# Linear attention's decays computed in pieces between the gates, sigmoids applied later, projections in another order

## The chip, the cores and the metric

The kernel runs on one core of a Trainium2 chip. The metric is the device time of one launch in microseconds (us). The engines are TensorE (PE in the profile; its weight loads are PEld), VectorE (DVE), ScalarE (ACT), GpSimd (POOL) and SyncE (SP), which issues most of the DMAs here.

## The reference

One layer of a streaming encoder on 16 meta tokens and 1024 frames, model width 1024, all in float32. The part around the change is the middle of it:

```
h += 0.5 * swiglu(rmsnorm(h))                       # first feed-forward block
u  = rmsnorm(h) * mix_norm
aq, ak, av, gq, gk, gv, gr, g_low, gate_a, gate_b = split(u @ w_in)
A  = window attention(aq, ak, av)                   # 8 heads, 2 kv heads, chunks of 64
log_a = log_sigmoid(g_low @ gla_gate_w + gla_gate_b) / 16
b  = cumsum(log_a) within a chunk                   # decays of linear attention
qe = gq/8 * exp(b);  ke = gk * exp(-b)
o  = causal(qe ke^T) v + qe S;   S' = exp(b_last) * S + (gk * exp(b_last - b))^T v
B  = rmsnorm(o) * silu(gr)
h += (sigmoid(gate_a) * (A @ Wa) + sigmoid(gate_b) * (B @ Wb)) @ w_out
h += 0.5 * swiglu(rmsnorm(h))                       # second feed-forward block; then a last rmsnorm
```

Linear attention has 4 heads with keys of 64 and values of 128. q, k and the decays are two tiles of 128 rows (two heads each, p = 0 and 1), gv and gr four tiles each, the gates sixteen.

## The kernel before

Everything is kept transposed: 128 features on the partitions, tokens along the free dimension. A float32 product is made of three matmuls, high x high, high x low and low x high, where "high" is the operand cast on ScalarE and "low" the rest, subtracted on VectorE (`split`, `Weights.cut`, `Seven.halves`).

The kernel is one program with unrolled loops. The tile framework orders it: it puts each engine's instructions into that engine's queue in an order of its own, by the program's order where operands are there, and derives the semaphores from the buffers. Each queue is worked off in order. A pool of tiles has a fixed count of buffers for a tag; a new tile waits until an old one's last reader is done.

The stages in order, by their lines:

1. The first feed-forward block, up to 704.7 us, in products of Strassen's kind with seven in place of eight (`Seven`, L453). Its last part is the loop at L819 to L848: for each half c of the tokens (520 each) and each of the eight tiles m, matmuls of the last hidden rows (L827) into a double PSUM bank, the residual sum `add_half` (L340, VectorE), a store, the square (L834, ScalarE) and the sum of squares (L836, VectorE or GpSimd). The norm's scale of the first half (`scales_of_half`, `scales_to_rows`) and the first scaled inputs (`scaled`, L807 to L811) lie within the second half's turns.
2. Plain projections. The PSUM pool of four double banks is closed and a pool of eight banks opened. `together` (L901) runs projections of several tiles and chunks of tokens side by side over the eight k tiles, with hooks between: K0, K1 and V0 of linear attention, and later V1. `ev_keep` copies a tile to DRAM, `ev_tok` copies a tile of V and later transposes it by tokens (L888, L892, on TensorE) and stores that. Between them VectorE makes the differences of tokens (L935 to L938) and their halves (L229) for the next stage.
3. Gates: `gate_pair` (L958) for m = 0, 2 to 14, again seven products of 12 matmuls of 512 columns each, into three accumulators (pb, pa, pd). Between the products, copies and sums take the accumulators out; a sigmoid on ScalarE (L973) follows and a store to `gates`.
4. Attention: its own projections first, then a loop over 16 chunks of 64 frames. Each turn has transposes of the probabilities, the scores of the next chunk with its softmax (VectorE, ScalarE, VectorE), a slot of filling work for TensorE, and the product with V. The slots hold V2 and V3, the two Q tiles and the four R tiles of linear attention, and the low-rank projection (`low_rank`) in slot 9.
5. Linear attention (`Gla`). `decays` (L1360 to L1391) for a whole head pair: z = gate matmul, Abs, Exp, Ln, the running sum (scan, L1373) and four more Exp, with products on VectorE and GpSimd. `begin` transposes the scaled keys (L1398, L1404), `products` (L1422), `step` (L1429 to L1443), `end`. Units of the attention branch (`branch_units`, 12 matmuls each, L96 to L98) fill the turns: five before the first head, then one in each turn of the first and in the even turns of the second as long as more than two are left. `out_gate` multiplies with Silu of gr.
6. The branch of linear attention (`ev_b`), the output projection, and the second feed-forward block.

Of the kernel before, what the change touches and what calls it, by code (L numbers as in the profile page):

```python
# [17 lines left out]
P = 128  # L18
D = 1024
KT = D // P  # L20
# [15 lines left out]
def hybrid_kernel(  # L36
# [13 lines left out]

    def bank(name="ps"):
        return psp.tile([P, 512], F32, tag="ps", name=name)
# [415 lines left out]
    dbl = {}  # L468
# [345 lines left out]
    wt = Weights([w_more, w_main, w_main], [r_main])  # L814
    plain_views = [cols_view(w_in, c) for c in (C_GK, C_GK + P, C_GV, C_GV + P)]
    raws = [wt.raw(v) for v in plain_views[0:2]]
    hw = [None] * 4
    dgs = {}
    for c in range(2):  # L819
        for m in range(KT):  # L820
# [12 lines left out]
            sq = sqs[m % 3][:, c * N1:(c + 1) * N1] if m else accs[c]  # L833
            nc.scalar.activation(sq, hm, AF.Square)  # L834
            if m:
                (nc.vector if c == 0 or m >= KT - 2 else nc.gpsimd).tensor_add(accs[c], accs[c], sq)  # L836
            if c == 0 and m in (1, 3):
                hw[m // 2] = ktiles(wt.cut(raws[m // 2], eng=nc.gpsimd))
            if c == 1:
                if m == 1:  # L840
                    raws.append(wt.raw(plain_views[2]))
# [36 lines left out]
    def ev_tok(i):  # L878

        def evac(ps, c0, n):  # L880
# [4 lines left out]
            def turn():  # L885
# [3 lines left out]
                nc.vector.tensor_copy(g[:, 0:fr * P], pt[:, 0:fr * P])  # L889
                nc.sync.dma_start(out=gv_dram[i, :, c0:c0 + fr * P], in_=g[:, 0:fr * P])  # L890
                if c0 + n == T:
                    nc.tensor.transpose(pt[0:NM, fr * P:fr * P + P], v[:, n - NM:n], ident)  # L892
                    nc.vector.tensor_copy(g[0:NM, fr * P:fr * P + P], pt[0:NM, fr * P:fr * P + P])
                    nc.sync.dma_start(out=gvm_dram[i], in_=g[0:NM, fr * P:fr * P + P])

# [3 lines left out]
    plain_evac = [ev_keep(gk_dram[0]), ev_keep(gk_dram[1]), ev_tok(0), ev_tok(1)]  # L899

    def together(tiles, chunks, hooks=()):  # L901

        pss = [(i, c0, n, bank("pj")) for i in tiles for c0, n in chunks]
# [9 lines left out]
        run_late()  # L913
        for i, c0, n, ps in pss:
            plain_evac[i](ps, c0, n)

    def second_scales():
        dgs[1] = scales_of_half(1, bank("tot"))

    hooks = {k: (lambda k=k: scaled(k, 0)) for k in range(3, KT)}  # L920
    hooks[2] = second_scales
    together([0, 1], CH_T[0:1], hooks)
    scales_to_rows(1, (bank("rep"), bank("rep")), dgs[1])
    for m in range(KT):
        scaled(m, 1)
    together([2], CH_T[0:1])
    together([0, 1, 2], CH_T[1:])
    ra.close()
    t_r = g7.enter_context(tc.tile_pool(name="tr", bufs=8, side="right"))
    g8 = Seven("mx", 512, lambda kind, which, turn: bank(f"p{kind}"), (t_r, t_g, blk, None, w_more), None, None, None, N1)  # L930
# [11 lines left out]
    hw[3] = ktiles(wt.cut(wt.raw(plain_views[3])))  # L942
    for ch in CH_T:
        together([3], [ch])
    run_late()
# [12 lines left out]
    def gate_pair(m):  # L958
# [13 lines left out]
        def keep(i, c, to, src):  # L972
            nc.scalar.activation(to, src, AF.Sigmoid)  # L973
            nc.sync.dma_start(out=gates[m + i, :, c * 512:(c + 1) * 512], in_=to)
# [7 lines left out]
        keep(0, 0, x11, x11)  # L982
# [7 lines left out]
        keep(1, 1, x22, x22)  # L990
        product(5)
        nc.vector.tensor_add(x12, d, x12)
        keep(0, 1, x12, x12)
        product(6)
        keep(1, 0, g8.block("x21"), b)
# [10 lines left out]
    wt.ws = [w_main]  # L1006

# [66 lines left out]


    GR = 2 * NM
    gw, glow = qp.tile([3 * GR, 256], F32R, name="gw"), qp.tile([P, T], F32R, name="glow")
    gwf = ttile("gwf")[0:3 * GR, 0:256]
    for i in range(6):
        nc.gpsimd.dma_start(out=gwf[i * NM:(i + 1) * NM, :], in_=gla_gate_w)  # L1080
    nc.scalar.copy(gw, gwf)
    nc.vector.tensor_sub(gw[2 * GR:, :], gwf[2 * GR:, :], gw[2 * GR:, :].bitcast(F32))

# [152 lines left out]

    def low_rank():
        raw = wt.raw(cols_view(w_in, C_GL, NM))
        w2 = w_main.tile([P, 1024], F32R, tag="w", name="w2", align_bytes=128)[:, 0:KT * 2 * NM].rearrange("p (k m) -> p k m", k=KT)
        rv = raw[:, 0:KT * NM].rearrange("p (k m) -> p k m", k=KT)  # L1240
        nc.scalar.copy(w2[:, :, 0:NM], rv)
        nc.vector.tensor_sub(w2[:, :, NM:2 * NM], rv, w2[:, :, 0:NM].bitcast(F32))
        for c0, n in CH_ALL:
            ps = bank("pj")
            for k in range(KT):
                nc.tensor.matmul(ps[0:2 * NM, 0:n], w2[:, k, :], u_hi[k][:, c0:c0 + n], start=(k == 0), stop=False)
                nc.tensor.matmul(ps[0:2 * NM, 0:n], w2[:, k, :], u_lo[k][:, c0:c0 + n], start=False, stop=(k == KT - 1))
            a = ps[0:GR, 0:n]
            hi = glow[0:GR, c0:c0 + n]
            nc.scalar.copy(hi, a)  # L1250
            nc.scalar.copy(glow[2 * GR:3 * GR, c0:c0 + n], a)
            nc.vector.tensor_sub(glow[GR:2 * GR, c0:c0 + n], a, hi.bitcast(F32))
# [5 lines left out]
    for i in range(2):  # L1258
        slots += [[u] for u in project_units(cols_view(w_in, C_GQ + i * P), CH_FR, ev_keep(gq_dram[i], 0.125))]
    for i in range(4):  # L1260
        slots += [[u] for u in project_units(cols_view(w_in, C_GR + i * P), CH_FR, ev_keep(gr_dram[i]))]
    slots[9].append(low_rank)
    values(0)
    cur = scores(0)
    held[0]()
    held[1]()
    for c in range(16):
        nxt = None
        turn(cur)
        if c < 15:  # L1270
            nxt = scores(c + 1)
        if c % 2 == 0 and c < 14:
            values(c // 2 + 1)
        for u in slots[c]:
            u()
        attend(cur)
        cur = nxt
    run_late()
    att.close()

# [26 lines left out]
    def load_a(m, c0, n):  # L1307
        g = ttile("ga")
        nc.sync.dma_start(out=g[:, 0:n], in_=gates[m, :, c0:c0 + n])
        return g  # L1310

    def ev_a(ps, m, c0, n, g):
        nc.vector.tensor_mul(g[:, 0:n], ps[:, 0:n], g[:, 0:n])
        nc.sync.dma_start(out=gates[m, :, c0:c0 + n], in_=g[:, 0:n])
# [3 lines left out]
    for m0 in range(0, KT, 2):  # L1318
        views = [(slice(g * 64, g * 64 + 64), lambda r: r.rearrange("p (k m) -> p k m", k=4),
                  w_branch_att[g * 256:(g + 1) * 256, m0 * P:(m0 + 2) * P].rearrange("(i d) m -> d i m", d=64)) for g in range(2)]  # L1320
        fill += branch_units(views, ya, m0, load_a, ev_a)

# [7 lines left out]
    for p in range(2):  # L1330
        for x, src, n in (("k", gk_dram[p], T), ("q", gq_dram[p], S), ("v", gv_dram[2 * p], S), ("w", gv_dram[2 * p + 1], S)):
            ins[x, p] = atile(f"g{x}{p}")
            nc.sync.dma_start(out=ins[x, p][:, 0:n], in_=src)
# [9 lines left out]
    reset = gp.tile([P, T], F32, name="reset", bufs=1)  # L1343
    nc.gpsimd.memset(reset, 1.0)
    nc.gpsimd.memset(reset.rearrange("p (a b) -> p a b", b=16)[:, 0:65:8, 0:1], 0.0)
    ssq = gp.tile([P, 2, 8, 2], F32, name="ssq", bufs=1)
# [373 lines left out]
```

## Time and profile before

| | |
|---|---|
| median of 3 runs | 2061.68 us (2061.63 to 2062.08) |
| profiled execution | 2064.81 us |
| its span, first to last instruction | 2063.1 us |
| mean granted TensorE clock | 0.987 |
| DMA | 334.62 MB, mean 162 GB/s |

The stages' bounds in the span are about 729.5 (first projection), 794.5 (first gate), 946.9 (attention's projections), 1003 (chunks), 1166.6 (linear attention) and 1266.6 us (its branch). In a table of stretches each row has the stretch, its length, then the busy time and the count of instructions of PE, PEld, DVE, ACT and POOL, the granted clock, the DMA share and the rate. A row of the waits has who waited, for whom, the sum in us, how often, and the longest. A row of a group has its line, engine, operation, out<-in with shapes and count, then busy us and mean ns, then the idle time before it with its releasers. Matmuls overlap in their pipeline, so a matmul's own duration is longer than the distance to the next one.

### The profile page before, as it was taken

The page shows a single profiled execution, that of the slowest core. Times are in us where ns is not written, and L with a number is a line of the kernel's source. Part 1 is how long each engine was busy: PE and PEld are TensorE (multiplying, and loading weights), DVE is VectorE, ACT ScalarE, POOL GpSimd, SP SyncE. Part 2 cuts the span into 40 slices and gives each one's busy share as a digit, 9 for nine tenths or more (in the row PEclk, how much of TensorE's full clock was granted, in tenths as well). Part 3 has the DMA queues.
Part 4 walks back from the last instruction along what each step waited for, and adds up shares of the span by engine and source line. Part 5 has one row for each costly group of instructions (what it writes and reads, how often), then busy time and mean ns, then how long its engine had stood idle before and what let it go on. Part 6 is the DMA issues. An engine that isn't in the chain of part 4 may idle for free.

```text
span 2063.1 us, 31910 instructions
## 1 busy us (share of the span) xinstructions
PE 2011.8 (98%) x12084; PEld 1784.1 (86%) x12084; DVE 1397.7 (68%) x2393; ACT 873.6 (42%) x1692; POOL 197.8 (10%) x216
## 2 busy tenths in 40 slices
PE   8899999999999999999999989999999999999998
PEld 8899999999999987888888767888888888878888
DVE  5866677676678785443466668668876776757885
ACT  5534444444322353433466635344544544442222
POOL 1000000001222110005000100120000000022212
PEclk9999999999999999999999989999999999999999
DMA  6333344349975323335111454741544443599822
GB/s 204 107 108 131 125 162 159 124 153 344 349 289 202 99 92 109 108 107 136 44 58 57 154 168 147 260 140 51 170 167 132 168 157 126 199 372 345 287 92 82
DMA packets 280874, 334.62 MB, mean 162 GB/s; under 512 B 25094, under 2 KB 190720, under 8 KB 280720
## 3 DMA queue, kind: packets, MB, share of 16 engines
q1 hardware_dynamic: 263072, 271.18, 39.8%
q10 hardware_dynamic: 17296, 61.29, 8.0%
q8 instruction: 95, 1.56, 0.3%
q14 instruction: 59, 0.48, 0.1%
q0 software_dynamic: 352, 0.11, 0.1%
HBM read 216.45 MB, written 116.06 MB: 161 GB/s over the span
## 4 chain that ended last, share of the span: by engine, by line
PE 87%; DVE 5%; DMA 4%; ACT 2%; issue 1%; POOL 0%; SPq 0%; DVEq 0%; POOLq 0%; ACTq 0%
PE pb L453 34%; PE pd L453 17%; PE pa L453 8%; PE pj L96 2%; PE pj L97 2%; PE pj L98 2%; PE wo L96 1%; PE wo L98 1%; PE wo L97 1%; PE br L96 1%; PE br L98 1%; PE br L97 1%; PE pd L827 1%; PE pg L628 1%; PE pg L630 1%
## 5 line engine op out<-in xcount | busy, mean ns | idle before, releaser
L453 PE MATMUL pb<-tt,wop 128*128 128x260 f32 (+1 forms) x2208 | 385.2, 327 | 0.0
L453 PEld LDWEIGHTS pb<-tt,wop 128*128 128x128 f32 x2208 | 330.9, 188 | 35.5
L229 DVE TENSOR_TENSOR wop<-s,wop 128x512 fp32r<-128x512 f32 x264 | 186.5, 713 | 113.3 <-ACT wop L228 112.7
L228 ACT CAST wop<-s 128x512 fp32r<-128x512 f32 x264 | 161.4, 622 | 226.0 <-PE pb L453 90.2
L453 PE MATMUL pb<-tm,wop 128*128 128x260 f32 (+1 forms) x1440 | 237.3, 321 | 7.1 <-DVE h L340 4.5
L453 PEld LDWEIGHTS pb<-tm,wop 128*128 128x128 f32 x1440 | 209.5, 190 | 27.2 <-DVE h L340 5.0
L228 ACT CAST wop<-raw 128x512 fp32r<-128x512 f32 x198 | 122.5, 623 | 223.6 <-PE pb L453 105.4
L229 DVE TENSOR_TENSOR wop<-raw,wop 128x512 fp32r<-128x512 f32 x198 | 139.5, 709 | 20.2 <-ACT wop L228 19.9
L436 POOL TENSOR_TENSOR s<-raw 128x512 f32<-128x512 f32 x28 | 37.1, 1326 | 1060.5 <-DMA tm<-f1mid 454.9
L453 PE MATMUL pd<-tt,wop 128*128 128x260 f32 (+1 forms) x768 | 136.4, 329 | 0.0
L453 PEld LDWEIGHTS pd<-tt,wop 128*128 128x128 f32 x768 | 115.9, 188 | 13.1
L340 DVE SCALAR_TENSOR_TENSOR h<-pb,h 128x520 f32<-128x520 f32 (+1 forms) x136 | 94.0, 693 | 39.8 <-PE pb L453 37.7
L453 PE MATMUL pd<-tm,wop 128*128 128x260 f32 (+1 forms) x720 | 118.8, 319 | 0.0
L453 PE MATMUL pb<-tb,wop 128*128 128x260 f32 (+1 forms) x672 | 112.3, 320 | 0.5 <-ACT vec L87 0.5
L453 PEld LDWEIGHTS pd<-tm,wop 128*128 128x128 f32 x720 | 104.3, 188 | 9.4
L453 PE MATMUL pd<-tb,wop 128*128 128x260 f32 (+1 forms) x672 | 112.2, 320 | 0.0
L453 PE MATMUL pa<-tb,wop 128*128 128x260 f32 (+1 forms) x672 | 112.0, 320 | 0.0
L453 PEld LDWEIGHTS pb<-tb,wop 128*128 128x128 f32 x672 | 97.9, 188 | 9.9 <-ACT vec L87 0.6
L453 PEld LDWEIGHTS pd<-tb,wop 128*128 128x128 f32 x672 | 97.9, 188 | 9.3
L453 PEld LDWEIGHTS pa<-tb,wop 128*128 128x128 f32 x672 | 97.8, 188 | 9.3
L436 DVE TENSOR_TENSOR s<-raw 128x512 f32<-128x512 f32 x94 | 64.6, 688 | 54.7 <-DMA raw<-in_ffn_w_up 52.6
L96 PE MATMUL pj<-uh,whi 128*128 128x512 f32 (+2 forms) x256 | 94.9, 371 | 0.0
(409 smaller groups left out, 4035.5 us busy)
## 6 DMA issues: line engine op xcount, KB each, us to landing
tm<-f1mid ACTq DMA_DIRECT2D x56, 520.0 KB, 6.6
tm<-f2mid ACTq DMA_DIRECT2D x56, 512.0 KB, 6.1
raw<-in_ffn_w_gate SPq DMA_DIRECT2D x42, 512.0 KB, 3.9
raw<-in_ffn_w_up SPq DMA_DIRECT2D x42, 512.0 KB, 4.0
raw<-in_ffn_w_down SPq DMA_DIRECT2D x80, 256.0 KB, 5.9
f1mid<-kh SPq DMA_DIRECT2D x70, 260.0 KB, 2.8
f1mid<-kl SPq DMA_DIRECT2D x70, 260.0 KB, 2.9
f2mid<-kh SPq DMA_DIRECT2D x70, 256.0 KB, 2.9
```

What stands on the lines that cost most here:

```text
L96: nc.tensor.matmul(ps, wh[k], xh[k], start=(k == 0), stop=False)
L97: nc.tensor.matmul(ps, wh[k], xl[k], start=False, stop=False)
L98: nc.tensor.matmul(ps, wl[k], xh[k], start=False, stop=(k == n - 1))
L228: nc.scalar.copy(x[:, 0:n], src)
L229: nc.vector.tensor_sub(x[:, n:2 * n], src, x[:, 0:n].bitcast(F32))
L340: nc.vector.scalar_tensor_tensor(hm, ps, 0.5, hm, op0=ALU.mult, op1=ALU.add)
L436: (eng.tensor_add if add else eng.tensor_sub)(a[s], a[x], a[y])
L453: nc.tensor.matmul(ps, y, z[:, s0:s0 + sn], start=(first and k == 0 and at == 0), stop=(at == 2 and k == len(cols) - 1), skip_group_check= ...
L628: nc.tensor.matmul(pss[i], wh, xh, start=(k == 0), stop=False)
L630: nc.tensor.matmul(pss[i], wl, xh, start=False, stop=(k == KT - 1))
L827: nc.tensor.matmul(ps, y, x[:, c0 + s0:c0 + s0 + sn], start=(n == 0), stop=(n == 3 * LAST - 1), skip_group_check=True)
```

## The change

- **PSUM.** The pool of four double banks stays open to the end of the gates' stage. Once the flag `open` is set, `bank` takes a double and hands out its two halves in turn.
- **Squares of the second half.** They get tiles of their own; the sums for m = 1 to 7 are made together on VectorE, in `second_scales`.
- **Order of projections.** The gates' stage gets K0, K1, Q0, Q1, R0 and the low-rank projection; all four V tiles go to the slots of the attention loop, with R1 to R3 and, in the last two slots, two units of the attention branch. Their weights are cut on VectorE.
- **Transposes of V.** The meta tokens' transpose comes ahead of the copy of the frames.
- **Decays.** `decay` works on a piece of 512 frames or of the 16 meta tokens of one head pair, after the gate pairs m = 2 to 12. It loads k and q, makes the four scaled arrays and stores them to DRAM; `Gla` loads them ready made. The products that GpSimd made are on VectorE.
- **Sigmoids.** The gates are stored raw; `ev_a` and `ev_b` apply the sigmoid when they are loaded. Silu in `out_gate` becomes a sigmoid and a multiplication.
- **Filling work.** Four units of the branch stand before the first head, then one in three turns of four as long as more than one is left.

```diff
     def bank(name="ps"):
-        return psp.tile([P, 512], F32, tag="ps", name=name)
+        if not dbl.get("open"):
+            return psp.tile([P, 512], F32, tag="ps", name=name)
+        if not spare:
+            both = double(name)
+            spare.extend([both[:, 512:], both[:, 0:512]])
+        return spare.pop()
...
-    hw[2] = ktiles(wt.cut(raws[2], eng=nc.gpsimd))
-    doubles.close()
-    psp = ctx.enter_context(tc.tile_pool(name="psp", bufs=8, space=PSUM))
+    dbl["open"] = True
...
     def second_scales():
+        for m in range(1, KT):
+            add_square(1, m)
         dgs[1] = scales_of_half(1, bank("tot"))
...
+    together([(0, CH_T[0]), (1, CH_T[0])], {k: (lambda k=k: scaled(k, 0)) for k in range(3, KT)})
+    hw[2] = ktiles(wt.cut(raws[2]))
+    together([(2, CH_T[0])], {4: second_scales})
+    hw[3] = ktiles(wt.cut(raws[3]))
+    together([(3, CH_T[0])], {4: lambda: scales_to_rows(1, (bank("rep"), bank("rep")), dgs[1])})
     for m in range(KT):
         scaled(m, 1)
+    together([(i, ch) for i in range(2) for ch in CH_T[1:]])
+    hw[4] = ktiles(wt.cut(wt.raw(plain_views[4])))
+    low_w = low_weights()
+    together([(2, CH_FR[1]), (3, CH_FR[1])])
...
+    for ch in CH_FR:
+        together([(4, ch)])
+    low_rank(low_w)
...
+    def decay(p, c0, n):
+        k, e, b = [g8.block(x)[:, 0:n] for x in ("k", "e", "b")]
+        nc.sync.dma_start(out=k, in_=gk_dram[p, :, c0:c0 + n])
+        bg = vec[:, GB + p:GB + p + 1]
+        ps = bank("z")[:, 0:n]
+        nc.tensor.matmul(ps, gw[:, p * P:(p + 1) * P], glow[0:3 * GR, c0:c0 + n], start=True, stop=True)
+        nc.scalar.activation(e, ps, AF.Abs, bias=bg)
+        nc.vector.tensor_scalar(b, ps, bg, 0.0, op0=ALU.add, op1=ALU.min)
+        nc.scalar.activation(e, e, AF.Exp, scale=-1.0)
+        nc.scalar.activation(e, e, AF.Ln, bias=1.0)
+        w = min(n, P)
+        for a in range(0, n, w):
+            nc.vector.tensor_tensor_scan(b[:, a:a + w], b[:, a:a + w], e[:, a:a + w], 0.0, op0=ALU.add, op1=ALU.subtract)
...
+        nc.scalar.activation(e, b, AF.Exp, scale=1.0 / 16.0)
+        nc.vector.tensor_copy(dec[p][:, c0 // P:(c0 + n) // P, :], by(e)[:, :, P - 1:P])
+        nc.vector.tensor_mul(e, q, e)
+        out("qi", e)
+        nc.vector.tensor_tensor(by(d), at(P - 1), by(b), op=ALU.subtract)
+        nc.scalar.activation(d, d, AF.Exp, scale=1.0 / 16.0)
+        nc.vector.tensor_mul(d, k, d)
+        out("kd", d)
...
+    pieces = [(p, c0, n) for p in range(2) for c0, n in CH_FR + [(S, NM)]]
     for m in range(0, 16, 2):
         if m == 14:
             g8.ring = [w_main] * 6
         gate_pair(m)
+        if 2 <= m <= 12:
+            decay(*pieces.pop(0))
...
+    doubles.close()
+    psp = ctx.enter_context(tc.tile_pool(name="psp", bufs=8, space=PSUM))
...
-    for i in (2, 3):
+    for i in range(4):
         us = project_units(cols_view(w_in, C_GV + i * P), CH_T, ev_tok(i))
         slots += [us[0:1], us[1:3]]
...
     def ev_a(ps, m, c0, n, g):
-        nc.vector.tensor_mul(g[:, 0:n], ps[:, 0:n], g[:, 0:n])
+        nc.scalar.activation(g, g, AF.Sigmoid)
+        nc.vector.tensor_mul(g, ps[:, 0:n], g)
...
-            nc.scalar.activation(a, a, AF.Silu)
+            nc.scalar.activation(g, a, AF.Sigmoid)
+            nc.vector.tensor_mul(a, a, g)
...
-    heads[0].decays()
-    for _ in range(5):
+    for _ in range(4):
         fill.pop(0)()
...
-            if j % 2 == 0 or p == 0:
-                if len(fill) > 2:
-                    fill.pop(0)()
+            if j % 4 != 3 and len(fill) > 1:
+                fill.pop(0)()
```

More of the change, by code (lines that the diff above doesn't have):

```diff
@@ L989, in gate_pair @@
         nc.vector.tensor_add(x22, b, x22)
-        keep(1, 1, x22, x22)
+        keep(1, 1, x22)
         product(5)
         nc.vector.tensor_add(x12, d, x12)
-        keep(0, 1, x12, x12)
+        keep(0, 1, x12)
         product(6)
-        keep(1, 0, g8.block("x21"), b)
+        x21 = g8.block("x21")
+        nc.scalar.copy(x21, b)
+        keep(1, 0, x21)
+    dec = [sml.tile([P, 8, 1], F32, tag="dec", name=f"dec{p}", bufs=2) for p in range(2)]
+    km_dram = dram.tile([2, P, NM], F32, name="km_dram")
@@ L1073, in hybrid_kernel @@
     build_bias()
[L1076 to L1082, printed above, removed]
     def ev_k(ps, c0, n):
@@ L1321, in hybrid_kernel @@
         fill += branch_units(views, ya, m0, load_a, ev_a)
+    slots += [[fill.pop(0)], [fill.pop(0)]]
+    values(0)
+    cur = scores(0)
+    held[0]()
+    held[1]()
+    for c in range(16):
+        nxt = None
+        turn(cur)
+        if c < 15:
+            nxt = scores(c + 1)
+        if c % 2 == 0 and c < 14:
+            values(c // 2 + 1)
+        for u in slots[c]:
+            u()
+        attend(cur)
+        cur = nxt
+    run_late()
+    att.close()
     gla = ExitStack()
```

202 lines of the change are left out of this document (90 added, 112 removed).

## The prediction

> **What bounds the kernel now.** I read the busy line of the page first, then a table of stretches between the parts of the program that the change touches, then TensorE's waits.
>
> ```profile
> PE 2011.8 (98%) x12084; PEld 1784.1 (86%) x12084; DVE 1397.7 (68%) x2393; ACT 873.6 (42%) x1692; POOL 197.8 (10%) x216
> ```
> ```profile
> core 0: us, PE busy (x) PEld busy (x) DVE busy (x) ACT busy (x) POOL busy (x), PEclk, DMA share, GB/s
> 729.50:794.50 65.00, 56.02 (x324) 49.11 (x323) 50.56 (x96) 29.66 (x68) 2.95 (x3) 0.89 0.25 86
> 794.50:946.90 152.40, 152.40 (x674) 126.14 (x673) 73.12 (x114) 65.31 (x112) 7.90 (x20) 1.00 0.39 116
> 1003.00:1166.60 163.60, 160.08 (x943) 134.37 (x942) 101.14 (x344) 99.76 (x292) 0.14 (x1) 1.00 0.22 66
> 1166.60:1266.60 100.00, 88.60 (x502) 65.99 (x501) 71.90 (x142) 50.65 (x115) 11.95 (x12) 0.91 0.47 154
> 1266.60:1310.00 43.40, 42.88 (x190) 34.93 (x189) 36.51 (x56) 15.86 (x24) 0.00 (x0) 1.00 0.73 242
> ```
> ```profile
> PE pj L910 <- issue: 4.6, 1, 4.6
> PE kv L1441 <- DVE o L1437: 4.3, 1, 4.3
> PE vt L888 <- ACT v L882: 3.8, 2, 3.2
> PE at L1422 <- issue: 2.6, 1, 2.6
> PE km L1398 <- DVE d L1385: 2.5, 1, 2.5
> PE vt L892 <- DVE g L889: 2.5, 2, 1.2
> ```
> ```profile
> 734.30:740.80 6.50, 6.44 (x23) 5.27 (x23) 3.75 (x7) 1.91 (x4) 0.00 (x0) 0.56 0.39 119
> 778.20:784.60 6.40, 6.35 (x15) 4.98 (x16) 0.93 (x2) 0.00 (x0) 0.00 (x0) 0.52 0.36 102
> 1186.90:1194.50 7.60, 6.88 (x22) 5.39 (x23) 5.28 (x11) 4.06 (x6) 0.00 (x0) 0.54 0.84 265
> 1205.40:1211.20 5.80, 5.06 (x16) 3.30 (x17) 5.63 (x11) 2.69 (x6) 2.36 (x1) 0.51 0.25 78
> ```
>
> TensorE is busy 98% of the span, so the change can win only the time in which it waits, and the time in which it works at half clock behind a wait. The second table, in order: plain projections (729.5 to 794.5), gates, attention, linear attention, its branch. The gates' stage has no idle TensorE. The plain projections lose 9.0 us, linear attention 11.4, attention 3.5. The last four rows show what follows a long wait: 6 to 8 us at a granted clock of 0.51 to 0.56, so that about half of their 26.3 us, 13, is lost as well.
>
> **The change part by part.** The matmuls stay the same in number and nearly in shape; they move. Their prices, as the distance between starts: 15 matmuls of 512 columns lie between the first pair of rows, and the chain has those of 256 and 272.
>
> ```profile
> 1057.75 0.39 PE L96 MATMUL pj<-uh,whi 128*128 128x512 f32 x1
> 1060.92 0.39 PE L98 MATMUL pj<-uh,wlo 128*128 128x512 f32 x1
> ...
> 787.91 0.12 PE pj L910
> 791.65 0.13 PE pj L910
> ```
>
> 3.17 / 14 is 0.227 us. A tile over all tokens is 24 x (0.227 + 0.12 + 0.125) = 11.3 us, one over the frames alone 48 x 0.227 = 10.9, the low-rank projection 16 x 0.472 = 7.5, a unit of the attention branch 12 x 0.227 = 2.7.
>
> *Plain projections.* Before: four tiles of 11.3 = 45.3, about 2 of transposes of V and 2 of the norm's small matmuls, 49.3; the stretch lasts 65.0, so 15.7 are lost. (The same from the rows: waits of 4.6, 3.8 and 0.6, and half of 12.9 us of slow clock, 15.4.) After: two tiles of 11.3, three of 10.9, 7.5 and 2, 64.9. The 15.6 us of new work would just fill the holes, if VectorE follows. It was busy 50.56 of the 65. From these rows
>
> ```profile
> L836 DVE TENSOR_TENSOR sums<-sums,sqs 128x520 f32<-128x520 f32 x2 | 1.4, 684 | 0.0
> L126 DVE TENSOR_TENSOR wlo<-raw,whi 128x1024 fp32r<-128x1024 f32 x3 | 3.9, 1295 | 1.4 <-ACT whi L125 1.4
> L889 DVE COPY g<-vt 128x512 f32<-128x512 f32 x2 | 1.4, 699 | 2.4 <-PE vt L888 2.4
> L889 DVE COPY g<-vt 128x256 f32<-128x256 f32 x4 | 1.7, 428 | 7.5 <-issue 7.5
> 733.46 0.69 DVE L340 SCALAR_TENSOR_TENSOR h<-pd,h 128x520 f32<-128x520 f32 x1
> 734.36 0.76 PE L910 MATMUL pj<-uh,whi 128*128 128x512 f32 x1 [4.57 <-issue]
> ```
>
> it gets five more adds of squares (3.4), two more cuts of weights (three where there was one, 2.6) and some 2 for the low rank, and loses 3.1 of copies of V: 55.5 of 64.9. It fits, but the scaling of both halves, the adds and the cuts come in a row ahead of the projections that need them. I take 2 us of new waiting, bounds 0 and 6. The wait at L910 has no named releaser. TensorE starts 0.2 us after the last evacuation from the old PSUM pool (L340, 733.46 + 0.69), so I read it as the change of pools. In the new order the first projection writes to a double bank that was emptied long before, and the seven adds come behind it.
>
> *Gates.* This stage gets six z matmuls (four of 512 and two small ones, 1 us, that leave linear attention) and the decays on ScalarE and VectorE.
>
> ```profile
> 1169.64 1.08 ACT L1370 ACTIVATE e<-e 128x1040 f32<-128x1040 f32 x1
> 1170.73 1.28 ACT L1371 ACT_TABLE_LOAD   x1
> 1172.03 1.07 ACT L1371 ACTIVATE e<-e 128x1040 f32<-128x1040 f32 x1
> ...
> L1373 DVE TENSOR_TENSOR_SCAN b<-reset,e 128x1040 f32<-128x1040 f32 x2 | 4.6, 2320 | 0.1
> L973 ACT ACTIVATE x<-x 128x512 f32<-128x512 f32 x24 | 15.2, 633 | 37.3 <-DVE x L989 21.6 <-DVE x L992 13.8 <-DVE x L980 1.8
> ...
> 815.97 0.39 PE L453 MATMUL pb<-uh,wop 128*128 128x512 f32 x1
> 816.39 0.59 ACT L978 COPY x<-pb 128x512 f32<-128x512 f32 x1 [2.12 <-PE pb L453]
> 818.91 0.39 PE L453 MATMUL pb<-tt,wop 128*128 128x512 f32 x1
> ```
>
> ScalarE: 65.3, less 24 sigmoids (15.2; the eight that read PSUM become copies), plus four pieces of seven functions at about 0.6 (17), two small ones (2) and two table loads of 1.28 a piece (15): 84 of 153. VectorE: 73.1 plus four times some 6.2 (scan 1.2, seven operations of 0.69 and a small one) and 1: 99. Neither becomes the bound by its sum. What can hurt is order: a product that adds to an accumulator waits until its last contents are copied. The copy ended at 816.98, the next matmul to pb came at 818.91, so a copy may be 1.9 us late for nothing. A table load and its function on half a row, 1.28 + 0.6, just fit; a queue head that waits for the scan behind them does not. Bounds 0 and 14 (2.3 for each of six pieces); I take 2.5, near the low end, since other work can be queued between and the load is within the slack. On the SyncE queue each large piece adds two loads and four stores of 256 KB: 6.3 MB in 153 us, 41 GB/s beside the 116 of the row, at a DMA share of 0.39. A store that waits for VectorE holds up the raw weights behind it; these are needed a pair, 19 us, later, so I set nothing for that.
>
> The Trainium skill ("ScalarE: Activation LUTs", What ACT_TABLE_LOAD costs and the section on table sets) puts a switch of tables at 2.66 us with its drain and tells one to do all functions of a set before switching; the change makes six groups of two. By 2.66 us the ScalarE sum would be 100. This trace has the next function 1.30 us behind the start of the load, so I go by that; what the drain would do is a rival below.
>
> *End of the gates.* The PSUM pool now changes here. TensorE has to wait for the last copy of pb: copy 0.6 and about 0.4 around it. Bounds 0.5 and 7.9 (the 4.6 of L910 and half of 6.5); I take 1, since neither ScalarE nor VectorE has decays left in the last pair.
>
> *Attention.* The filling work goes from V2, V3, two Q, four GR and the low rank (22.7 + 2 + 21.8 + 43.6 + 7.5 = 97.6) to four V, three GR and two units of the branch (45.3 + 4 + 32.7 + 5.4 = 87.4): 10.2 less, which is work that has moved. The transposes of the meta tokens come ahead of VectorE's copy, so the 2.5 us at L892 goes. The last two slots have 2.7 us of filling work instead of 5.4, behind a softmax that goes VectorE, ScalarE, VectorE, and each unit has a sigmoid there. New waits between 0 and 7 (twice the missing 2.7 and one table load); I take 3, the middle, since later units can be pulled in.
>
> *Linear attention.* Without the decays nothing remains of what VectorE did between 1180 and 1211: the waits at L1398, L1422 and L1441 go with their slow clock (9.4 idle, 0.6 of small ones, half of 13.4: 16.5). Its loads are twelve in place of eight; they stand on the SyncE queue ahead of the branch's weights and gates, as the eight do now, and start when the projections end, two slots earlier than now.
>
> ```profile
> gw<-gv_dram SPq DMA_DIRECT2D x2, 512.0 KB, 7.3
> ```
>
> The fourth of a group lands 7.3 us after its issue, so the six of the first head take about 11, against two slots and four units (over 20 us) until they are needed: nothing. What is late next is the end:
>
> ```profile
> 1258.99 0.49 PE L1432 MATMUL go<-st,qi 64*128 64x128 f32 x4
> 1264.99 0.38 PE L1463 MATMUL ot<-ident,o 128*128 128x128 f32 x2
> ```
>
> Between the last step and the output transposes lie 6.0 us, covered by two units of 2.7. One unit is left, and VectorE gets a multiplication of 0.69 for each of eight pieces of the output gate. New waits 0 to 9; I take 4. In the branch of linear attention behind it, each unit of 2.7 us of TensorE gets a sigmoid of 0.63 on a ScalarE busy a third of the time: nothing.
>
> Sum: 15.7 + 2.5 + 16.5 = 34.7 removed; 2 + 2.5 + 1 + 3 + 4 = 12.5 new; the moved work cancels (+15.6 + 1 - 10.2 - 5.4 - 1 = 0). Net 22.2 us. The profiled span of 2063.1 becomes 2040.9; that execution took 2064.8 in all, the median of the runs is 2061.7, so the forecast on the median's scale is 2039.5, say 2040. A change of under 0.2%, about 4 us, could not be told from none.
>
> **The rivals.**
>
> *VectorE stays the bound of the projections.* For it: for 25 us of this stretch it never rested, as the third busy time (VectorE's) of this row says, and its list gets longer.
>
> ```profile
> 753.00:778.00 25.00, 21.50 (x164) 20.40 (x162) 25.00 (x46) 14.05 (x30) 0.00 (x0) 0.99 0.31 113
> ```
>
>  Against it: 9 us to spare in the sum. A wait of 6 us there in place of 2, and half of a slow stretch of 6.5 us behind it, is 7 more; with the tail of attention at its upper bound (4 more) 11: 2047 to 2051.
>
> *The pool's wait stays,* since L910 waited for something else (scaled inputs from VectorE). The change then does not do there what it says: 4.6 + 3.3 remain, 2048.
>
> *The decays block the accumulators.* This ends slower. Each piece would do to TensorE what the second head's decays did at L1441: 4.3 us of idle and half of 5.8 at a low clock, 7.2. Six pieces give 43 in place of 2.5, net 18 us slower: 2080. It decides from 4.1 us a piece on (22.2 + 2.5 over six). For it: that very wait is a copy behind decays in VectorE's queue. Against it: pieces of half the width, no GpSimd multiplications beside them, an accumulator pipeline with 1.9 us of slack and a second and third bank to go on with.
>
> *The drain behind a table load.* A load with its function that holds ScalarE for 3.3 us in place of 1.9 exceeds the slack by 1.4 in each of 12 switches: 17 us, 2057. The trace speaks against it, by the 1.30 us above. It is the price by the Trainium skill's page on ScalarE named above.
>
> *Hardly any new wait.* The program order leaves room to pull work in everywhere: 2027 to 2031.
>
> **How the numbers follow.** Forecast (2031 to 2046) 0.57; VectorE or the pool's wait 0.17; hardly any wait 0.12; blocked accumulators 0.10, of which 0.01 near zero; the drain 0.04, half of it within 0.2%. The predicted time is the forecast's, 2040. The range 2030 to 2056 leaves out the blocked accumulators, half of the drain and about half of the case without waits. Faster by over 0.2%: 0.57 + 0.17 + 0.12 + 0.02 = 0.88; within 0.2%: 0.03; slower: 0.09.
>
> **What would show it.** No wait over 1.5 us and a granted clock of 1.00 in the projections; a gates' stage of 154 to 157 us; no wait at the steps of linear attention but some 3 us ahead of the output transposes. I am wrong if gates' products wait for copies of pb, pa or pd for more than 10 us in all, if the first projection still waits 4 us, or if TensorE runs slow in the last slots of attention.

## The result and the profile after

The changed kernel takes 2083.62 us (median of 4 runs, 2082.20 to 2084.47) beside 2061.82 for the kernel before on the same chip (2061.63 to 2062.08): 1.0105 times as long, 95% interval 1.0087 to 1.0122. The forecast was 2040, in a range of 2030 to 2056. The profiled execution took 2084.47, its span is 2082.8.

The busy line of the page after, then the same stretches as before, cut at the same events, and TensorE's waits. Accumulators that share a double bank carry the name of the bank's first user here, so z and pa are accumulators of the gates too.

```profile
PE 2014.3 (97%) x12084; PEld 1782.2 (86%) x12084; DVE 1401.3 (67%) x2441; ACT 890.3 (43%) x1727; POOL 177.9 (9%) x205
```
```profile
core 0: us, PE busy (x) PEld busy (x) DVE busy (x) ACT busy (x) POOL busy (x), PEclk, DMA share, GB/s
730.20:794.90 64.70, 64.11 (x339) 52.57 (x338) 47.19 (x92) 30.04 (x70) 3.07 (x7) 1.00 0.34 109
794.90:995.40 200.50, 168.59 (x696) 132.50 (x694) 101.22 (x174) 88.96 (x145) 5.01 (x14) 0.91 0.38 119
995.40:1051.80 56.40, 55.74 (x292) 48.15 (x292) 18.39 (x27) 17.03 (x32) 22.49 (x58) 1.00 0.34 92
1051.80:1207.20 155.40, 150.11 (x938) 130.70 (x936) 103.07 (x349) 99.67 (x289) 0.00 (x0) 0.99 0.30 96
1207.20:1289.00 81.80, 78.42 (x476) 58.69 (x475) 48.09 (x123) 37.03 (x106) 1.15 (x7) 0.98 0.45 155
1289.00:1333.00 44.00, 44.00 (x195) 36.45 (x194) 37.05 (x57) 24.12 (x39) 0.00 (x0) 0.99 0.70 227
```
```profile
PE z L460 <- ACT wop L235: 17.2, 4, 8.4
PE pa L460 <- ACT wop L235: 13.1, 2, 6.6
...
PE tp L1304 <- DVE p L1289: 5.3, 3, 4.5
...
PE ot L1512 <- DVE o L1500: 2.2, 2, 1.2
```

The rows in order: projections, gates, attention's projections, attention, linear attention, its branch. Cut at the same events, these lasted 64.7, 152.7, 55.4, 164.0, 100.3 and 44.6 us before. Five of the six did about what was forecast. The gates alone grew by 47.8 us, more than all that the rest won. Of that row 200.50 - 168.59 = 31.9 us are idle TensorE, and the granted clock is 0.91. If each matmul of the stage took the median distance to the next start that its shape has in this trace, the stage would take 155.1 us; so 45.4 are lost, 31.9 of them idle and the other 13.5 for the most part at the low clock behind the waits, as in this row behind the longest one:

```profile
851.20:857.60 6.40, 6.40 (x17) 4.66 (x18) 4.79 (x8) 3.75 (x7) 0.00 (x0) 0.60 0.58 151
```

The two first rows of the waits above name what TensorE lacked: `wop` cast at L235. Those are not accumulators to be emptied; they are the *weights* of the next pair, which `Seven.halves` casts on ScalarE.

Where the weights were, in the timelines of VectorE and ScalarE in the third pair of the changed kernel (start, duration, engine, line, operation; in brackets the idle time before it). TensorE stood from 842.8 to 851.2:

```profile
834.36 0.69 DVE L1039 TENSOR_TENSOR x<-pa,x 128x512 f32<-128x512 f32 x1 [1.96 <-PE pa L460]
838.29 0.75 DVE L1058 TENSOR_SCALAR b<-z,vec 128x512 f32<-128x512 f32 x1 [3.24 <-ACT e L1057]
842.18 1.37 DVE L1064 TENSOR_TENSOR_SCAN b<-b,e 128x128 f32<-128x128 f32 x4 [3.14 <-ACT e L1061]
...
848.47 0.69 DVE L1094 TENSOR_TENSOR k<-k,e 128x512 f32<-128x512 f32 x1
849.07 0.69 DVE L443 TENSOR_TENSOR s<-raw 128x512 f32<-128x512 f32 x1
```
```profile
837.56 0.69 ACT L1057 ACTIVATE e<-z,vec 128x512 f32<-128x512 f32 x1
838.28 1.28 ACT L1060 ACT_TABLE_LOAD   x1
839.57 0.63 ACT L1060 ACTIVATE e<-e 128x512 f32<-128x512 f32 x1
840.22 1.28 ACT L1061 ACT_TABLE_LOAD   x1
841.51 0.63 ACT L1061 ACTIVATE e<-e 128x512 f32<-128x512 f32 x1
843.63 1.28 ACT L1080 ACT_TABLE_LOAD   x1 [1.48 <-DVE b L1064]
...
850.52 2.18 ACT L235 CAST wop<-s 128x512 fp32r<-128x512 f32 x4 [2.78 <-DVE s L443]
```

The same place in VectorE's timeline of the kernel before:

```profile
829.99 0.69 DVE L992 TENSOR_TENSOR x<-pd,x 128x512 f32<-128x512 f32 x1 [1.96 <-PE pd L453]
830.60 0.68 DVE L436 TENSOR_TENSOR s<-raw 128x512 f32<-128x512 f32 x1
```

Before, the four sums of the next pair's raw weights (L436; L443 after) come right behind the pair's last evacuation. After, a whole decay piece stands between the two. Its last product starts at 848.47. With the piece at the head of its queue VectorE is idle for 3.24 and 3.14 us, waiting for ScalarE, and ScalarE for 1.48, waiting for the scan. The sums follow at 849.07, the casts at 850.52, 7.7 us after TensorE stopped for them. The Trainium skill ("PSUM — Partial Sum Buffer", Engine vs sequencer instructions) states that the queues of ScalarE, VectorE and GpSimd are strictly first in, first out. This trace agrees: the sums wait through 6.4 us in which VectorE has nothing to do.

### The profile page after: what moved, and what is told of

Read it like the earlier page. It is cut to its first block, busy times and chain, and to the rows that moved or that the text cites. A ratio compares the mean times of both kernels' runs of the same rounds, so it can differ in the third digit from the quotient of the medians.

```text
span 2082.8 us, 32065 instructions
## 1 busy us (share of the span) xinstructions
PE 2014.3 (97%) x12084; PEld 1782.2 (86%) x12084; DVE 1401.3 (67%) x2441; ACT 890.3 (43%) x1727; POOL 177.9 (9%) x205
## 4 chain that ended last, share of the span: by engine, by line
PE 89%; DMA 3%; ACT 3%; DVE 3%; issue 1%; SPq 0%; DVEq 0%; ACTq 0%; POOLq 0%
PE pb L460 30%; PE pd L460 16%; PE pa L460 9%; PE z L460 3%; PE pj L103 2%; PE pj L104 2%; PE pj L105 2%; PE br L103 1%; PE wo L103 1%; PE wo L105 1%; PE wo L104 1%; PE br L104 1%; PE br L105 1%; DMA f1mid<-kh 1%; PE pd L841 1%
## 5 line engine op out<-in xcount | busy, mean ns | idle before, releaser
L460 PE MATMUL pb<-tt,wop 128*128 128x260 f32 (+1 forms) x2040 | 343.5, 322 | 0.0
L460 PEld LDWEIGHTS pb<-tt,wop 128*128 128x128 f32 x2040 | 299.3, 188 | 29.0
L235 ACT CAST wop<-s 128x512 fp32r<-128x512 f32 x264 | 162.1, 621 | 241.2 <-PE pb L460 95.7
L236 DVE TENSOR_TENSOR wop<-s,wop 128x512 fp32r<-128x512 f32 x264 | 184.7, 708 | 89.2 <-ACT wop L235 88.6
L235 ACT CAST wop<-raw 128x512 fp32r<-128x512 f32 x198 | 122.4, 623 | 235.3 <-PE pb L460 105.2
L236 DVE TENSOR_TENSOR wop<-raw,wop 128x512 fp32r<-128x512 f32 x198 | 139.5, 710 | 28.3 <-ACT wop L235 27.8
L443 POOL TENSOR_TENSOR s<-raw 128x512 f32<-128x512 f32 x28 | 37.1, 1324 | 1057.2 <-DMA tm<-f1mid 454.8
L460 PE MATMUL pd<-tt,wop 128*128 128x260 f32 (+1 forms) x708 | 121.2, 324 | 0.1
L460 PEld LDWEIGHTS pd<-tt,wop 128*128 128x128 f32 x708 | 104.6, 188 | 11.2 <-DVE wop L236 0.6
L443 DVE TENSOR_TENSOR s<-raw 128x512 f32<-128x512 f32 x94 | 64.6, 688 | 56.6 <-DMA raw<-in_ffn_w_up 54.9
L347 DVE SCALAR_TENSOR_TENSOR h<-pd,h 128x520 f32<-128x520 f32 (+3 forms) x112 | 72.6, 654 | 33.7 <-PE pd L460 17.5
```

Source lines behind the costliest of these rows:

```text
L235: nc.scalar.copy(x[:, 0:n], src)
L236: nc.vector.tensor_sub(x[:, n:2 * n], src, x[:, 0:n].bitcast(F32))
L347: nc.vector.scalar_tensor_tensor(hm, ps, 0.5, hm, op0=ALU.mult, op1=ALU.add)
L443: (eng.tensor_add if add else eng.tensor_sub)(a[s], a[x], a[y])
L460: nc.tensor.matmul(ps, y, z[:, s0:s0 + sn], start=(first and k == 0 and at == 0), stop=(at == 2 and k == len(cols) - 1), skip_group_check= ...
```

## The experiments

Theory: the place of the decays in the two queues is the cause, ahead of something that TensorE needs soon. Rivals: ScalarE and VectorE simply have too much to do in this stage; or the function tables cost too much as such; or the double PSUM banks are handed back too late. All times are beside the kernel before, which took 2061.5 to 2062.8 us on these chips.

**Sums ahead of the decay.** The raw weights are fetched and summed before the piece (`gate_raws`: the loads, the `Group` and its `sums`); the casts stay where they were.

```diff
+    following = gate_raws(0)
     for m in range(0, 16, 2):
-        gate_pair(m)
+        gate_pair(m, following)
+        if m < 14:
+            following = gate_raws(m + 2)
         if 2 <= m <= 12:
             decay(*pieces.pop(0))
```

> The changed kernel, but each pair of gates loads its weights and makes their four sums (L443) one pair early, so that in the program they stand ahead of the decays of the pair before. Theory A (queue order: TensorE waits because the sums of the next weights stand behind the whole piece of decays in VectorE's queue): the six waits in the gates' stage (31 us with the small ones) and the slow clock behind them (13 us) go, the stage takes 153 to 157 us instead of 199, the kernel 2037 to 2045 us. Theory B (ScalarE is held up by the decays' functions and their table loads, so that the casts of the weights come late whatever the order): the waits stay at over half, the stage takes over 175 us, the kernel over 2060. Theory C (the double PSUM banks are handed back too late): no change, 2080 to 2085.

2076.45 us (1.0067, 1.0044 to 1.0090), gates 194.8. TensorE's waits in it, and ScalarE's timeline behind a pair:

```profile
PE pa L460 <- ACT wop L235: 17.0, 4, 4.7
...
PE z L460 <- ACT x L1029: 5.1, 6, 2.1
```
```profile
837.91 1.28 ACT L1064 ACT_TABLE_LOAD   x1
839.20 0.63 ACT L1064 ACTIVATE e<-e 128x512 f32<-128x512 f32 x1
839.74 0.60 ACT L235 CAST wop<-s 128x512 fp32r<-128x512 f32 x1
840.25 1.13 ACT L235 CAST wop<-raw 128x512 fp32r<-128x512 f32 x2
841.40 1.28 ACT L1083 ACT_TABLE_LOAD   x1
```

The longest wait falls from 8.4 to 4.7, and the kernel gets 7 us back, no more. The theory that the sums alone are late falls: now the casts stand among the decay's functions and table loads. In addition accumulators (x at L1029) begin to wait. Stage and time are those set down for theory B; whether the casts would come late whatever the order, as B says, is left to the runs below that move them too.

**Sums preferred by the scheduler,** by a priority of 200 steps: `with tc.high_priority(offset=200): g.sums(nc.vector)`.

> The changed kernel, but the scheduler is told to prefer the four sums wherever they can be placed; the order in which tiles take their buffers stays. In VectorE's queue the sums then stand behind the second difference of the decays (L1089) instead of behind its last product (L1094), four products of 0.69 us earlier. Theory A, order of preference alone: no waits are left, near 2040 us. Theory A, buffers (the sums share a tag with the decays' tiles and take their buffers after them): each of the four long waits (8.4, 6.6, 6.4, 7.4 us) becomes some 4 us shorter and stays long enough for the slow clock, the stage falls from 199 to about 180 us, the kernel to 2062 to 2070. Theory B: no change to speak of, over 2078.

2086.11 us (one run), gates 201.4, where theory A had about 180 and at most 2070. There are six waits for weights of 23.3 us in sum, and six of 6.4 in sum for VectorE's sum of the second product (x at L1027), which now stands behind the preferred sums. One wait became two. Why the sums were not placed further ahead is not shown, and this edit settles nothing by itself.

**No logarithm,** so that no table has to change within a piece. This kernel leaves the logarithm out, so its decays are other numbers.

```diff
-        nc.scalar.activation(e, e, AF.Ln, bias=1.0)
+        nc.scalar.activation(e, e, AF.Exp, scale=-1.0)
```

> The changed kernel with the Ln of the decays replaced by another Exp (the log of the decay is left out, so the decays are others); the order of the queues stays nearly the same, but the tables need not be switched. By the traced 1.28 us a load, theory A: each long wait becomes 2.6 to 3.8 us shorter, since the chain ahead of the sums does, and is 4 to 5 us long still; the kernel falls by 12 to 18 us to 2066 to 2072. Theory B with the 2.66 us a switch of the Trainium skill (ScalarE: Activation LUTs, What ACT_TABLE_LOAD costs): over 5 us for each, next to no long wait is left, under 2055.

2072.01 us (one run), gates 189.4. The row of its gates' stage:

```profile
791.80:981.20 189.40, 168.04 (x696) 132.48 (x694) 100.95 (x174) 74.01 (x134) 5.03 (x15) 0.94 0.40 126
```

ScalarE is busy 88.96 - 74.01 = 15.0 us less, twelve loads of 1.28 (the stage has 13 in the changed kernel and one here), and the stage is 11.1 us shorter. So by this run the loads are about a quarter of the 45.4 us; they lengthen the piece. 34 remain without them, and 2072 is the upper end of what theory A had set down. The Trainium skill ("ScalarE: Activation LUTs", Rules for kernel authors) says to do all functions of one set before switching. By this run that would win some 11 us here, an estimate, and not the stage.

**Decays back in linear attention,** low-rank projection too; all else of the change stays (PSUM pool, order of projections, sigmoids, filling work).

```diff
-    low_rank(low_w)
...
-        if 2 <= m <= 12:
-            decay(*pieces.pop(0))
...
+    slots[9].append(low_rank)
...
+    heads[0].decays()
```

> The changed kernel with the decays back in the stage of linear attention as before, and the low-rank projection back in slot 9 of attention; the order of the projections, the PSUM pool, the late sigmoids and the filling work stay as changed. Theory A: the gates' stage takes 152 to 154 us; the plain projections have no wait over 1.5 us and no slow clock; linear attention has its three long waits again (12 us idle and half of 13 at slow clock); 2046 to 2052 us. If the projections' part gains nothing (the kernel before only lost there what now shows elsewhere): 2058 to 2064.

2067.23 us (1.0024, 1.0013 to 1.0035). The rows of linear attention, the projections and the gates, and two waits of linear attention:

```profile
1166.80:1271.20 104.40, 86.61 (x482) 63.58 (x480) 72.55 (x144) 68.52 (x136) 13.04 (x12) 0.87 0.33 112
727.70:786.70 59.00, 58.43 (x307) 49.34 (x306) 48.50 (x93) 30.31 (x69) 3.07 (x7) 1.00 0.34 114
786.70:944.80 158.10, 154.45 (x673) 125.28 (x671) 72.60 (x112) 50.09 (x89) 4.98 (x14) 1.00 0.37 112
```
```profile
PE km L1419 <- DVE d L1406: 7.9, 1, 7.9
...
PE go L1450 <- DVE o L1458: 4.6, 1, 4.6
```

The gates fall to 158.1, so the decays with their z are what costs them 42 us. The projections keep their gain (59.0 us without the low rank, clock 1.00). But linear attention takes 104.4, where it took 81.8 without the decays and 100.3 before, there with one more unit of filling work ahead of the first head.

The time lies above both ranges that I had set for this run. Besides linear attention the gates are over what I expected: 158.1 is 5.4 more than before, without any decay, with four waits of 0.7 us for the copy of the first product (x at L993) and smaller ones. So the rest of the change costs the gates something too; by what, was not tested.

**Weights ahead.** Raw weights and sums of the next pair come after this pair's second product, and all seven casts as this pair's products go by (the last lines stand in `product`, behind the product itself). The first pair's weights are made ahead of the stage, and the last pair's casts stay where they were. The piece stays at the pair's end.

```diff
         nc.vector.tensor_add(x11, a, x11)
-        g.sums(nc.vector)
         keep(0, 0, x11)
+        if m < 14:
+            nxt[0] = gate_raws(m + 2)
...
+            if i >= 2 and m < 12:
+                while len(h.ws) <= i:
+                    h.ws.append(h.weights(len(h.ws)))
```

> Edit: each pair of columns' raw weights are fetched and summed after the second product of the pair before, and all seven operands are cast as that pair's products go by; the decay piece stays at the end of the pair, so in both queues it now stands behind every weight of the next pair but the last one or two. If only the weights' place behind the decays costs (sums and casts), the four waits of 6.4 to 8.4 us go: gates 154 to 160 us, kernel 2038 to 2046. If the accumulators are the next thing to wait (the evacuations of the first products stand behind the piece's 12.6 us chain on ScalarE and VectorE, and the third product adds to the bank that the first one's evacuation reads, 5.4 us into the pair), four waits of 4 to 7 us stay, now at the third or fourth product and for an evacuation: gates 172 to 185, kernel 2056 to 2068. If ScalarE and VectorE are simply too full in this stage, the sum of the lost time stays as in the changed kernel, about 45 us.

**Piece early.** The same, and the piece starts whole after the second product's sum (`hook(m)` behind `keep(0, 0, x11)`), no longer at the end.

> As the run with the weights ahead, but each decay piece is started whole after the second product's sum, 5.4 us into a pair. The next pair's sums and casts are behind it in both queues but not needed for another 13 us or more. Theory of the place alone (weights): gates 154 to 160, kernel 2038 to 2046. Theory of the accumulators: the evacuation of the third product stands behind the chain and the fifth product adds to its bank from 10.9 us on, so a wait of about 6 us at each of the four large pieces at the fifth product: gates 175 to 185, kernel 2058 to 2068. Theory of occupancy: lost time about 45 us as before.

**Halves.** As the last, with the piece cut in two behind the scan; the second half (four Exp and their products) follows one pair later.

```diff
+        return b
+
+    def decay_rest(p, c0, n, b):
...
+    def hook(m):
+        if begun:
+            decay_rest(*begun.pop())
+        else:
+            now = pieces.pop(0)
+            begun.append((*now, decay(*now)))
```

> As the run with the piece started early, but in two halves of about 5 us each, a pair apart: logarithm and running sum after the second product of one pair, the four exponentials and products after the second product of the next. Each half lies between two evacuations that the accumulators can spare (2.7 us of slack), and ahead of nothing that is needed within 10 us. If the order in the two queues is the whole cause: gates 153 to 160 us, the kernel 2034 to 2046, below the kernel before. If ScalarE and VectorE are too full, or the reloading of function tables costs as such: gates over 175 and the kernel over 2058.

Weights ahead took 2060.53 us (0.999, 0.998 to 1.000), piece early 2071.98 (1.0044, 1.0029 to 1.0059), halves 2052.60 (0.9954, 0.9937 to 0.9970). The waits of the three within the gates, in this order:

```profile
PE z L460 <- ACT x L1038: 8.2, 4, 3.5
...
PE pa L460 <- DVE wop L236: 3.5, 2, 3.0
```
```profile
PE pd L460 <- ACT x L1047: 23.8, 6, 5.7
```
```profile
PE pd L460 <- ACT x L1047: 6.6, 3, 4.1
...
PE pb L460 <- DVE x L1040: 2.9, 3, 1.5
```

And the stage's row in halves:

```profile
792.40:962.70 170.30, 160.63 (x695) 128.43 (x694) 96.42 (x166) 86.33 (x141) 4.98 (x14) 0.99 0.42 134
```

With the weights ahead the gates take 179.3 us, as expected if the accumulators are next: 21 of the 45 lost are gone. What waits now is mostly the first product's evacuation (x at L1038) behind the piece, shorter than expected (3.5 at most, where 4 to 7 stood), and twice still a last weight (L236). Started early, the piece holds up the third product's evacuation (L1047) instead, up to 5.7 us, at the small pieces too (1.6), and the stage takes 190.6, more than the 175 to 185 that I expected. Both are the waits that the theory of the accumulators named, at its two places. In halves the same functions on the same engines (96.42 and 86.33 us busy, in a stage 30 us shorter than the changed kernel's; some 5 us of VectorE's work, the first pair's weights, now lie ahead of the stage) leave 15.2 us lost. Its 170.3 lies between the two ranges that I had set, 153 to 160 for order as the whole cause and over 175 for too much to do, so it speaks against the second without settling it. The longest wait left, 4.1, is at the first of the two places where a large half and a 16-column piece with four table loads come together; at the second it is 1.5.

**Small pieces apart:** the two 16-column pieces come after the fourth product of the fourth and eighth pair, the halves stay after the second product.

```diff
         nc.scalar.copy(x22, d)
+        hook_small(m)
```

**Halves after the fourth product,** and the 16-column pieces after the second, the other way round:

```diff
         keep(0, 0, x11)
-        hook(m)
+        hook_small(m)
...
         nc.scalar.copy(x22, d)
+        hook(m)
```

> As the run in halves (2052.6, gates 170.4, one wait of 4.06 us where a large half and a 16-column piece came together with four table loads, others of 0.7 to 1.7), but the two 16-column pieces go into two other places, after the fourth product of the fourth and eighth pair. If what still waits is only what stands in ScalarE's queue between two evacuations, the 4.06 us wait goes with the slow clock behind it: gates 163 to 167, kernel 2045 to 2050. If it is the number of table loads, it moves to the new place and the time stays at 2051 to 2054.

> As the run in halves, but each half starts after the evacuation of the fourth product, where ScalarE has no evacuation to make until the seventh product's, 8 us later, instead of after the second product, 2.7 us ahead of the next one; the two 16-column pieces stand after the second product of the fourth and eighth pair. If the evacuations behind a half are what waits: every wait of a second accumulator's evacuation on ScalarE goes, VectorE's evacuation of the fifth product may wait up to 2 us for a half's products; gates 156 to 163, kernel 2038 to 2046. If it is the load on the two engines wherever it stands: 170 and 2050 to 2054 as in halves.

Small pieces apart took 2049.38 us (0.9937, 0.9921 to 0.9954), gates 167.2, about as expected: the wait of 4.1 fell to 1.7. Halves after the fourth took 2051.55 (0.9952, 0.9938 to 0.9967), gates 172.1, a miss; its time is the one set down for the load on the two engines. The first halves left only 0.5 us there, a second half holds up VectorE's sum of the fifth product (x at L1052) by 0.8, and each small piece after the second product costs 2.2, the longest of each row here:

```profile
PE pb L460 <- DVE x L1040: 3.8, 2, 2.2
...
PE z L460 <- ACT x L1047: 2.2, 1, 2.2
```
```profile
819.87 0.69 DVE L443 TENSOR_TENSOR s<-raw 128x512 f32<-128x512 f32 x1 [2.74 <-DMA raw<-in_w_in]
```

The other 1.6 us of the first row, up to 823.75, are no half's: the sum of the second product stands behind the sums of the raw weights, and VectorE had waited 2.74 us for their transfer.

**Mixed:** first halves after the fourth product, second halves after the second, small pieces after the fourth of the fourth and eighth pair.

> The first halves (two table loads) after the evacuation of the fourth product, where they left waits of 0.5 us, the second halves after the second product, where they left 0.7 to 0.8 us (after the fourth 0.8 to 1.6, on VectorE), and the 16-column pieces after the fourth product of the fourth and eighth pair, where no wait was seen behind them. If each of the two engines waits only for what stands just ahead of an evacuation in its own queue, the waits left are three or four of 0.5 to 0.8: gates 160 to 165, kernel 2042 to 2048. If it is the load wherever it stands, 167 to 172 and 2049 to 2053 as in the two runs before.

2046.77 us (0.9932, 0.9919 to 0.9946): faster than both kernels. Time and stage lie within what was expected from the order alone, and below what was expected from the load. Its gates' row, and its largest wait for an evacuation in that stage:

```profile
792.20:955.70 163.50, 159.15 (x696) 127.12 (x694) 95.45 (x166) 86.12 (x142) 5.04 (x15) 1.00 0.44 138
```
```profile
PE pb L460 <- DVE x L1040: 1.7, 2, 1.0
```

Here the same work costs the stage 163.5 - 152.7 = 10.8 us where the changed kernel pays 47.8. So the larger part of its loss, 37 us, is the order in the two queues. That is the end of the theory that the engines have too much to do, of the one that table loads cost so much as such (there are still 13), and of the one about the PSUM banks, which are the same.

## Why the prediction was wrong

By its own terms, in us, between the same events in both traces:

| step | forecast | measured |
|---|---|---|
| projections: -15.7 lost, +15.6 moved in, +2 new | +1.9 | 0.0 |
| gates: +1 of z, +2.5 new | +3.5 | **+47.8** |
| end of the gates, change of pools | +1.0 | +1.0 |
| attention: -10.2 moved, -2.5, +3 new | -9.7 | -8.6 |
| linear attention: -5.4 and -1 moved, -16.5, +4 new | -18.9 | -18.5 |
| ahead of these and behind them | 0 | -2.0 |
| span | -22.2 | +19.7 |

*Projections, right.* The low-rank work and the new order fill the holes; the clock is 1.00 and no wait over 1.5 us is left. The wait at the first projection is gone, so the rival that the pool's wait stays falls, and VectorE (47.19 us busy of 64.70) is not the bound.

*End of the gates, attention, linear attention, right.* At the end of attention the wait for the softmax is there (L1304, 5.3 in sum). Ahead of the output transposes it is 2.2, where I took 4 in all.

*Gates, wrong.* The failed step is the one that set 2.5 us for new waiting, within 0 and 14. Its sums held: ScalarE was forecast at 84 us and was busy 88.96, VectorE at 99 and 101.22, and neither is the bound. What failed is the sentence "What can hurt is order: a product that adds to an accumulator waits until its last contents are copied". It asked who waits for the two engines and named the accumulators alone. The second user stood in the code: four sums and seven casts with their subtractions for each pair, on the same two queues. The prediction looked at their raw operands on the SyncE queue, found them "needed a pair, 19 us, later" and set nothing, and never followed them on. "Other work can be queued between" was the other half of the error: what was queued was the work that TensorE needed, and it stood behind.

*The slack was compared with the wrong length.* 1.9 us of slack was held against one load and one function. What holds a queue up is the whole piece from the first function to the last product, 837.56 to 849.16, 11.6 us, since ScalarE and VectorE hand it to and fro. The run with the piece early shows that the accumulators would have waited as well, 4.5 to 5.7 us at each large piece, so even the wait that was considered had too low an upper bound (2.3 a piece).

*The rival that decays block the accumulators* came out nearly to the figure: 7.2 us a piece, 43 in all and 2080, against 45.4 lost and 2083.6. That the price fits is luck. It was six pieces of 7.2; the trace has four waits of 6.4 to 8.4 us at the large pieces, with some 3 more lost behind each (13.5 over four), and waits of 0.4 to 0.9 at the two small ones. Its resource did not hold: in the changed kernel the weights come late first, and the accumulators are next (shown by weights ahead). A chance of 0.10 was too little, above all since the wait at L1441 in the trace of before had shown this very thing.

*The other rivals fall.* The drain behind a table load is not there: the next function starts 1.29 us behind the load's start (838.28 and 839.57), as in the trace before. The Trainium skill ("ScalarE: Activation LUTs", What ACT_TABLE_LOAD costs) gives 2.66 with its drain, which this trace does not bear out. Hardly any new wait is contradicted by the gates.

*What stays open.* The best order found still loses 8.3 us in the gates, in waits of 0.5 to 1.0 and what follows them, where 2.5 was forecast; without the difference 2040 would nearly have been reached. The stage without any decay, in the run with the decays back, was only 5.4 us shorter than this one and itself 5.4 longer than before. Where that part comes from, and whether an order without these waits exists, was not tried.

## What to carry to other kernels

Before work is put on an engine that feeds or empties TensorE, list everything that this engine does for the next 20 us, and ask of each item what stands ahead of it in the queue; busy time that fits says nothing about that. Count a chain that goes to and fro between two engines by its length from end to end, for each queue that it occupies, and cut it into parts shorter than the slack, behind the weights that are needed next. When one wait is removed, name the next one at the same place and price it before counting the gain.

## What the runs showed that I had not expected

A wait of TensorE can cost a stretch at low clock as well as itself, and its length alone does not say whether it does. In the runs' gates' stages every wait of 2.2 us or more was followed by five us at a granted clock of 0.69 or less. In weights ahead one of 2.64 (911.8 to 914.5) was, and so was one of 1.43 (up to 939.07) that came 1 us behind another of 0.56. In small pieces apart one of 1.72 (886.6 to 888.3) was not:

```profile
914.50:919.50 5.00, 5.00 (x15) 4.00 (x16) 5.00 (x9) 2.53 (x5) 0.00 (x0) 0.66 0.70 262
939.10:944.10 5.00, 5.00 (x15) 3.97 (x16) 4.97 (x9) 1.99 (x4) 0.00 (x0) 0.66 0.70 264
```
```profile
888.34:893.34 5.00, 5.00 (x22) 4.15 (x23) 3.17 (x6) 1.58 (x3) 0.00 (x0) 1.00 0.46 135
```

In sums ahead of the decay a wait of 1.79 was followed by 0.66 and one of 2.08 by 1.00, so no single limit lies between. In the mixed order the waits are 1.0 us or less and the stage's clock is 1.00. It is not shown that many short waits are better than one long one of the same sum: halves and halves after the fourth have 9.7 and 9.5 us of idle TensorE in the stage, and the first, with the longer single wait, is 1.8 us the shorter.
